# Gate and up of the first FFN by seven block products instead of eight, with weights split late

## The chip, the cores and the metric

The kernel runs on one core of a Trainium2 chip. A core has five engines that run side by side, each with an instruction queue of its own that it works off in order: TensorE (PE, matmuls), VectorE (DVE), ScalarE (ACT), GpSimd (POOL) and SyncE (SP, which issues transfers here). The metric is the device time of one execution in microseconds (us); lower is better.

## The reference

A backbone of two layers over 768 tokens (256 of context, 512 latent) with 1024 features. Layer 0 mixes the tokens by gated linear attention and differential attention side by side, layer 1 by a Mamba-2 SSD mixer on all tokens; each layer then runs a SwiGLU FFN with 2816 hidden features. Everything is fp32. The part that is changed most is the FFN of layer 0:

```python
def swiglu(h, w_in, w_out):
    gate, up = jnp.split(h @ w_in, 2, axis=-1)
    return (jax.nn.silu(gate) * up) @ w_out
...
mod_x = jax.nn.silu(c) @ mod_w[layer] + mod_b[layer]      # latent tokens
mod_c = jax.nn.silu(c_ctx) @ mod_w[layer] + mod_b[layer]  # context tokens
...
x = layer_norm(ALPHA * x + gf_x * swiglu(x * (1.0 + scf_x) + shf_x, ffn_w_in[layer], ffn_w_out[layer]),
               ln_g[layer, 1], ln_b[layer, 1])
```

The context tokens go through the same formulas with their own modulation; after layer 1 only the latent tokens are needed.

## The kernel before

**Products.** An fp32 product is three matmuls on operands that are split in a high and a low part (hi x hi, hi x lo, lo x hi; `mm3`). The activations stand split in R (768 tokens, 8 blocks of 128 features). A weight comes by a DMA of 512 KB (128x1024) into one of three buffers RAW; ScalarE copies it to the high part, and VectorE or GpSimd subtracts this from RAW to give the low part, both in RW, which has room for four weights. `issue_loads` issues the DMAs and the splits whenever `free` gives room back, and `take` hands out the next weight.

**Order.** Nothing is put in order by hand. The class `Timing` (`tm`) keeps planned times of each engine and places each instruction in them; `tm.either` puts an elementwise operation on VectorE or GpSimd, where it ends first by the plan. Side work is written as chains (Python generators, `spawn`), which `pump` lets go on between matmuls, and `need` runs a chain to its end. The program's order on each engine is the order of the planned times. All instructions are issued through one helper, so that all have line 105 in the profile; groups are told apart by their tiles.

**The FFN of layer 0** (`ffn`) has 22 hidden chunks of 128 features. `hidden(c)` computes a chunk (`gated`): gate for two groups of 384 tokens, each 8 blocks x 3 matmuls of 128x384, then up in the same way, 96 matmuls; Silu on ScalarE, the product with up on VectorE out of the PSUM tile PS, then the split of the result into the slots f. Chunks are taken in groups of three (the last of four). After a group, `out_partial` computes its part of the output product: 6 token tiles x 2 halves x 3 chunks x 3 matmuls of 128x512, 108 in all, each sum added from PS to the accumulator in HB by VectorE. The first chunk of the next group stands ahead of a group's output product.

**Beside it** run three things. The norm of the mixer's output is finished on entry (`finish`: gain and bias, 128x1024 each, for six token tiles). The modulation of layer 1 is summed (`mod_sums`: for three groups of 2048 columns, 128x1024 weights times a column of c on VectorE, once for the latent and once for the context tokens, then summed over partitions by matmuls with ONE). And late in the FFN the residual of each tile is prepared (`ln.prep`: input times ALPHA by ScalarE, gates, one 128x1024 operation), ahead of the last output product, into which the next layer's norm is woven. In layer 1's mixer the residuals are prepared in one go by the entry "p" of its order, ahead of the last quarter of the output projection.

Of the kernel before, what the change touches and what calls it, by code (L numbers as in the profile page):

```python
# [11 lines left out]
F32 = mybir.dt.float32  # L12
# [206 lines left out]
def backbone(ctx: ExitStack, tc: tile.TileContext, ins: dict, out: bass.AP):  # L219
# [20 lines left out]
    HB = pool.tile([P, NU * U], F32, name="HB")  # L240
    RAW = pool.tile([P, 3, 1024], F32, name="RAW")
    HX = pool.tile([P, 2, 1024], F32, name="HX")
# [3 lines left out]

    def unit(i, n=U):
        return HB[:, i * U:i * U + n]

# [69 lines left out]
    def pump():  # L319
        going = True  # L320
# [43 lines left out]
    plan = []  # L364
    wgate = {}
    wq = {"loaded": 0, "issued": 0, "taken": 0, "freed": 0}
    wviews = {}

    def plan_cols(key, w, c0, n=P):
        plan.append((key, [(None, w[:, c0:c0 + n].rearrange("(k p) c -> p k c", p=P))], (KD, n)))  # L370

    def plan_rows(key, w, k):
        plan.append((key, [(None, w[k * P:(k + 1) * P, :].unsqueeze(1))], (1, D)))

    def plan_halves(key, n, w, c0):
        for i in range(2):
            plan.append(((key, n, i), [(None, w[i * 512:(i + 1) * 512, c0:c0 + 256].rearrange("(k p) c -> p k c", p=P))], (4, 256)))

    def issue_loads(limit=None):
        limit = limit or len(plan)  # L380
        while wq["loaded"] < min(limit, wq["issued"] + 3):
            j = wq["loaded"]
            _, pieces, (a, b) = plan[j]
            rv = RAW[:, j % 3, 0:a * b].rearrange("p (a b) -> p a b", b=b)
            for sl, ap in pieces:
                dma(rv[:, :, sl] if sl is not None else rv, ap)
            wq["loaded"] += 1
        if wq["issued"] < min(limit, wq["freed"] + 4):
            j = wq["issued"]
            _, _, (a, b) = plan[j]  # L390
            r = RAW[:, j % 3, 0:a * b]
            i = j % 4
            hi, lo, hf = RW[:, i, 0:a * b], RW[:, 4 + i, 0:a * b], RWf[:, i, 0:a * b]
            if plan[j][0] in wgate:
                tm.either(r, r, wgate[plan[j][0]], ALU.mult)
            S.activation(hi, r, AF.Copy)
            tm.either(lo, r, hf, ALU.subtract)
            wviews[j] = hi.rearrange("p (a b) -> p a b", b=b), lo.rearrange("p (a b) -> p a b", b=b)
            wq["issued"] += 1
            issue_loads(limit)  # L400

    def take(key):
        j = wq["taken"]
        assert plan[j][0] == key, (plan[j][0], key)
        wq["taken"] += 1
        return wviews[j]

    def free(n=1):
        wq["freed"] += n
# [128 lines left out]
    def mod_sums(l, g, accs, slots, bank, tbank, pace):  # L538

        mod_bias(l, g)  # L540
        for k in range(KD):
            for hf in range(2):
                r = slots[ring("ms", len(slots))]
                c0 = g * 2048 + hf * 1024
                dma(r, mod_w[l, k * P:(k + 1) * P, c0:c0 + 1024])
                yield pace
                for m in range(2):
                    a, c = accs[2 * m + hf], CST[:, 2 * k + m:2 * k + m + 1]
                    if k == 0:
                        S.activation(a, r, AF.Copy, scale=c)  # L550
                    else:
                        V.scalar_tensor_tensor(a, r, c, a, ALU.mult, ALU.add)
        yield tuple(accs)
        o = PS[:, bank, :]
        for m in range(2):
            for j in range(4):
# [1276 lines left out]
```

## Time and profile before

| | |
|---|---|
| median of 3 runs | 2034.73 us (2030.9 to 2034.9) |
| profiled execution | 2033.6 us |
| span of its trace | 2031.7 us |
| mean granted clock of TensorE | 0.978 of full speed |
| TensorE busy | 1921.0 us |
| VectorE busy | 1352.5 us |
| ScalarE busy | 783.8 us |
| GpSimd busy | 224.5 us |

The span is the time from the first to the last instruction in the trace of one execution. A timeline row reads: start, length, engine, line, operation, tile written <- tiles read, shape, count, and in brackets the idle time before it with what ended it. A row of grouped instructions reads: group and count, then total busy time and the mean of one in ns, then the idle time before them and what ended it. RW <- RAW,RW is the low part of a weight, RW <- RAW its high part, f <- HB,f the low part of a hidden chunk, HB <- HB,CST the modulation sums, and HX <- PS,GB the modulated activations before they are split into R.

### The profile page before, as it was taken

How to read it: one execution, taken by the hardware profiler on the slowest of the kernel's cores; microseconds unless marked ns; L12 is line 12 of the kernel's file. 1: busy time of each engine (PE TensorE's matmuls, PEld its weight loads, DVE VectorE, ACT ScalarE, POOL GpSimd, SP SyncE). 2: the span in 40 equal slices, each digit the busy share in tenths (PEclk: the TensorE clock that was granted, in tenths of full speed). 3: DMA queues.
4: the chain of work that ended last, by engine and by line, in shares of the span. 5: the costliest groups of instructions: out<-in, count | busy, mean ns of one | idle time of the engine just before them, and what ended most of it. 6: DMA issues, size and time to landing. Idle time of an engine off the chain costs nothing.

```text
span 2031.7 us, 27248 instructions
## 1 busy us (share of the span) xinstructions
PE 1921.0 (95%) x10660; PEld 1650.1 (81%) x10660; DVE 1352.5 (67%) x2065; ACT 783.8 (39%) x1494; POOL 224.5 (11%) x281
## 2 busy tenths in 40 slices
PE   7999999997899999999998999999899789999997
PEld 4878787966899989899886888788788678888886
DVE  4765645588815656666478988977978884444456
ACT  3523135445423122212135465655546443222232
POOL 0100000021300000000113321401102230000010
PEclk9999999999999999999998999999999799999999
DMA  8433411122424434434323432233333325333331
GB/s 284 126 126 115 138 42 32 53 63 73 147 72 145 137 113 147 134 114 154 105 78 101 105 91 87 73 89 89 102 96 94 116 82 173 97 103 94 94 119 58
DMA packets 233071, 216.37 MB, mean 107 GB/s; under 512 B 18869, under 2 KB 202807, under 8 KB 232943
## 3 DMA queue, kind: packets, MB, share of 16 engines
q1 hardware_dynamic: 232943, 214.64, 34.4%
q8 instruction: 83, 1.36, 0.3%
q14 instruction: 45, 0.37, 0.1%
HBM read 204.94 MB, written 9.67 MB: 106 GB/s over the span
## 4 chain that ended last, share of the span: by engine, by line
PE 75%; DVE 14%; issue 3%; DMA 3%; ACT 3%; POOL 1%; SPq 0%; POOLq 0%; DVEq 0%; ACTq 0%
PE PS L105 75%; DVE HB L105 8%; DVE RW L105 2%; ACT HB L105 2%; DVE l L105 1%; DMA HB<-acs_rows 1%; DVE LNS L105 1%; ACT RW L105 1%; DMA HB<-in_x_dram 1%; DVE HX L105 1%; DVE sml L105 0%; SPq L105 0%; POOL HB L105 0%; DVE R L105 0%; POOL LNS L105 0%
## 5 line engine op out<-in xcount | busy, mean ns | idle before, releaser
L105 PE MATMUL PS<-R,RW 128*128 128x384 f32 (+3 forms) x5184 | 987.3, 349 | 19.9 <-DVE HB L105 5.8
L105 PEld LDWEIGHTS PS<-R,RW 128*128 128x128 f32 (+1 forms) x5184 | 887.3, 189 | 106.0 <-issue 20.6
L105 DVE TENSOR_TENSOR RW<-RAW,RW 128x1024 fp32r<-128x1024 f32 (+1 forms) x204 | 255.8, 1270 | 217.4 <-ACT RW L105 216.7
L105 ACT ACTIVATE RW<-RAW 128x1024 fp32r<-128x1024 f32 (+1 forms) x222 | 228.8, 1046 | 237.5 <-issue 174.5
L105 PE MATMUL PS<-RW,f 128*128 128x512 f32 x1320 | 304.7, 390 | 1.9 <-DVE RW L105 1.5
L105 ACT ACTIVATE HB<-PS 128x512 f32<-128x512 f32 (+4 forms) x247 | 129.8, 533 | 428.0 <-PE PS L105 409.7
L105 PEld LDWEIGHTS PS<-RW,f 128*128 128x128 f32 x1320 | 247.0, 188 | 55.0 <-DVE RW L105 2.1
L105 DVE TENSOR_TENSOR HB<-PS,HB 128x512 f32<-128x512 f32 (+2 forms) x276 | 160.2, 587 | 92.3 <-PE PS L105 88.7
L105 PE MATMUL PS<-RW,R 128*128 128x256 f32 (+1 forms) x1440 | 200.7, 298 | 5.4 <-DVE HB L105 4.1
L105 ACT ACTIVATE HB<-HB 128x128 f32<-128x128 f32 (+4 forms) x372 | 159.9, 488 | 102.6 <-DVE HB L105 67.5
L105 PEld LDWEIGHTS PS<-RW,R 128*128 128x128 f32 x1440 | 186.8, 196 | 14.1 <-DVE HB L105 4.9
L105 PE MATMUL PS<-RW,l 128*128 128x512 f32 x576 | 157.5, 415 | 15.5 <-DVE HX L105 6.8
L105 DVE TENSOR_TENSOR HB<-HB 128x256 f32<-128x256 f32 (+3 forms) x191 | 151.2, 802 | 21.8 <-ACT HB L105 16.3
L105 PE MATMUL PS<-HB 128*128 128x128 f32 (+6 forms) x896 | 147.2, 353 | 10.2 <-DVE HB L105 7.6
L105 PEld LDWEIGHTS PS<-RW,l 128*128 128x128 f32 x576 | 105.1, 192 | 45.5 <-DVE HX L105 8.2
L105 PEld LDWEIGHTS PS<-HB 128*128 128x128 f32 (+3 forms) x896 | 100.9, 188 | 42.5 <-DVE HB L105 12.7
L105 ACT ACTIVATE f<-HB 128x384 fp32r<-128x384 f32 (+2 forms) x68 | 37.4, 550 | 236.5 <-DVE HB L105 236.4
L105 POOL TENSOR_TENSOR HB<-HB 128x256 f32<-128x256 f32 (+1 forms) x55 | 72.8, 1334 | 504.8 <-DVE HB L105 336.1
L105 DVE TENSOR_TENSOR HB<-HB,PS 128x384 f32<-128x384 f32 (+2 forms) x68 | 39.7, 584 | 106.2 <-PE PS L105 106.2
L105 DVE SCALAR_TENSOR_TENSOR HB<-HB,CST 128x1024 f32<-128x1024 f32 x84 | 105.0, 1277 | 0.0
L105 DVE SCALAR_TENSOR_TENSOR HB<-HB,CW 128x770 f32<-128x770 f32 (+1 forms) x96 | 102.0, 1066 | 3.0
L105 PE MATMUL PS<-ident,HB 128*128 128x128 f32 x480 | 76.8, 288 | 22.5 <-DVE HX L105 11.5
(145 smaller groups left out, 1297.8 us busy)
## 6 DMA issues: line engine op xcount, KB each, us to landing
RAW<-in_ffn_w_in_dram SPq DMA_DIRECT2D x88, 512.0 KB
HB<-in_mod_w_dram SPq DMA_DIRECT2D x48, 512.0 KB
RAW<-in_ffn_w_out_dram SPq DMA_DIRECT2D x44, 512.0 KB
RAW<-in_ssd_w_in_dram SPq DMA_DIRECT2D x40, 512.0 KB
mod<-in_mod_w_dram SPq DMA_DIRECT2D x72, 256.0 KB
HB<-acs_rows SPq DMA_DIRECT2D x64, 256.0 KB
RAW<-in_ev_w_in_dram SPq DMA_DIRECT2D x20, 512.0 KB
RAW<-in_ssd_w_out_dram SPq DMA_DIRECT2D x16, 512.0 KB
```

Source lines behind the costliest of these rows:

```text
L105: f(*a, **k)
```

## The change

1. In layer 0's FFN, gate and up of the chunks 4 to 21 are computed together as a 2x2 block product: blocks of the weights are 512 input features x 128 columns of gate or up, blocks of the activations 512 features x 384 tokens. `sevenths` runs seven products of 4 blocks x 3 matmuls of 128x384 in place of eight, and combines them: three copies out of PS by ScalarE (g0, u1, g1), additions by VectorE, then Silu, product and split as before. Products 1, 5, 6, 3, 7, 2, 4 run in this order in three banks a chunk, two sets in turn.
2. Of the seven weight blocks three are blocks as loaded; four (5, 6, 3, 7) are sums or differences, built by `factor` in TW and a piece of HB. All seven are split on their own, 128x512 each. The sums of the activation blocks are built and split once (`input_sums`) into TX and a tile "sums"; the lower third of HB becomes a tile HA in the same slot, which gives place to "sums" in the FFN.
3. RW is a ring of eight single units, of which a whole weight takes two. A split that is not yet due (within two or three weights of its use) is issued only when the plan shows ScalarE and VectorE idle; `issue_loads` is asked at each `pump`.
4. The norm's finish and the input sums run as a chain (`prologue`). The residuals are prepared one by one: in layer 0 by a chain `preps`, on which the last output product waits tile by tile, in layer 1 right ahead of each tile of the last quarter of the output projection.
5. `mod_sums` takes weights of 128x512 and sums the context tokens' row in the first group only, which holds the shift and scale ahead of layer 1's mixer; the context rows of the other two groups enter nothing.

```diff
+    FACTORS = "1563724"
...
+    def plan_pair(key, w, c0, c1):
+        for c in (c0, c1):
+            j = load(w[:, c:c + P].rearrange("(k p) c -> p k c", p=P), (KD, P))
+        for f in FACTORS:
+            items.append(((key, f), 1, j, f))
+    def factor(f, j):
+        w = [[RAW[:, (j - 1 + i) % 3, k * 512:(k + 1) * 512] for k in range(2)] for i in range(2)]
+        if f in "124":
+            return {"1": w[0][0], "2": w[0][1], "4": w[1][1]}[f]
+        r = TW[f in "67"]
+        a, b, op = {"5": (w[1][0], w[1][1], ALU.add), "6": (TW[0], w[0][0], ALU.subtract),
+                    "3": (w[0][1], TW[1], ALU.subtract), "7": (w[0][0], w[1][0], ALU.subtract)}[f]
+        tm.either(r, a, b, op)
+        return r
...
-        if wq["issued"] < min(limit, wq["freed"] + 4):
...
+            late = n >= max(upto, wq["taken"] + (2 if f is None else 3))
...
+                if late and not idle(r, *v):
+                    return
...
-        for k in range(KD):
-            for hf in range(2):
-                r = slots[ring("ms", len(slots))]
-                c0 = g * 2048 + hf * 1024
-                dma(r, mod_w[l, k * P:(k + 1) * P, c0:c0 + 1024])
+        for js, ms in ((((0, 1), (0, 1)), ((2, 3), (0, 1))) if g == 0 else (((0, 1, 2, 3), (0,)),)):
+            for k in range(KD):
+                for i, j in enumerate(js):
+                    r = slots[ring("ms", len(slots))]
+                    c0 = g * 2048 + j * 512
+                    dma(r, mod_w[l, k * P:(k + 1) * P, c0:c0 + 512])
...
+        def sevenths(c):
+            n = ring("sets", 2)
+            o1, o2, o3 = (PS[:, 3 * n + i, 0:N2] for i in range(3))
...
+            prod("1", o1, True)
+            S.activation(g0, o1, AF.Copy)
+            prod("5", o3, True)
+            S.activation(u1, o3, AF.Copy)
+            prod("6", o1)
+            S.activation(g1, o1, AF.Copy)
+            prod("3", o3)
+            V.tensor_tensor(g1, o3, g1, ALU.add)
+            S.activation(g1, g1, AF.Silu)
+            prod("7", o1)
+            V.tensor_tensor(u1, o1, u1, ALU.add)
+            tm.either(u1, u1, g1, ALU.mult)
+            store(u1, slice(N2, 2 * N2))
+            prod("2", o2, True)
+            V.tensor_tensor(g0, o2, g0, ALU.add)
+            S.activation(g0, g0, AF.Silu)
+            need(*sums)
+            prod("4", o1)
+            V.tensor_tensor(g0, o1, g0, ALU.mult)
+            store(g0, slice(0, N2))
...
-        for t in tiles:
-            lnin.finish(t)
+        def prologue():
+            for t in tiles:
+                lnin.finish(t, l == 0)
+                if l == 0:
+                    yield 2.4
+            if l == 0:
+                yield from input_sums(True)
...
-                        for t in tiles:
-                            ln.prep(t)
+                        def preps():
+                            for t in tiles:
+                                ln.prep(t)
+                                prepped.add(t)
+                                yield 4.0
...
-                for t in range(2, NT):
-                    ln.prep(t)
...
+                    if i == 3:
+                        ln.prep(t)
```

A product "6", "3" or "7" goes into a bank without clearing it (`start` false), so it adds to what the product before left there.

What stands in the engines' queues at the places that the prediction speaks of follows; the numbers behind tile names are buffer numbers. TensorE, around a chunk of layer 0's FFN, before (f are the hidden chunks in an output product, R_69 the split activations):

```order
L105 MATMUL PS<-RW,f_4_3787 128x512 x3
L105 MATMUL PS<-RW,f_0_3783 128x512 x3
L105 MATMUL PS<-R_69,RW 128x384 x249
L105 MATMUL PS<-HB,ONE 32x512 x8
L105 MATMUL PS<-R_69,RW 128x384 x9
```

And after, from the end of an output product on:

```order
L105 MATMUL PS<-RW,f_0_3780 128x512 x3
L105 MATMUL PS<-R_69,RW 128x384 x12
L105 MATMUL PS<-TX,RW 128x384 x12
L105 MATMUL PS<-sums_4057,RW 128x384 x12
L105 MATMUL PS<-R_69,RW 128x384 x12
L105 MATMUL PS<-sums_4057,RW 128x384 x12
L105 MATMUL PS<-R_69,RW 128x384 x36
L105 MATMUL PS<-TX,RW 128x384 x12
```

One long run over several chunks has become products of 12: 1, 5, 6, 3, 7, then 2, 4 and the next chunk's 1 as one row of 36.

VectorE in the same chunks, before:

```order
L105 TENSOR_TENSOR HB<-HB,PS 128x384
L105 TENSOR_TENSOR f_0_3783<-HB,f_0_3783 128x384
L105 SCALAR_TENSOR_TENSOR HB<-HB,CST 128x1024
L105 TENSOR_TENSOR HB<-HB,PS 128x384
L105 TENSOR_TENSOR f_0_3783<-HB,f_0_3783 128x384
L105 TENSOR_TENSOR RW<-RAW,RW 128x1024
```

And after (HB<-RAW, TW<-HB,RAW and HB<-RAW,TW are block sums of weights):

```order
L105 TENSOR_TENSOR HB<-RAW 128x512
L105 TENSOR_TENSOR TW<-HB,RAW 128x512
L105 TENSOR_TENSOR RW<-HB,RW 128x512
L105 TENSOR_TENSOR RW<-TW,RW 128x512
L105 TENSOR_TENSOR HB<-RAW,TW 128x512
L105 TENSOR_TENSOR HB<-PS,HB 128x384
L105 TENSOR_TENSOR RW<-HB,RW 128x512
L105 SCALAR_TENSOR_TENSOR HB<-HB,CST 128x512
L105 TENSOR_TENSOR HB<-PS,HB 128x384
L105 TENSOR_TENSOR HB<-HB 128x384
L105 SCALAR_TENSOR_TENSOR HB<-HB,CST 128x512
L105 TENSOR_TENSOR f_1_3781<-HB,f_1_3781 128x384
```

More and smaller operations stand between those that read PS.

VectorE at the entry of layer 0's FFN, where HX <- PS,GB is awaited by TensorE, before:

```order
L105 BN_STATS LNS<-HB 128x6
L105 TENSOR_TENSOR RW<-RAW,RW 128x1024 x2
L105 TENSOR_SCALAR HX<-PS,GB 128x128
```

And after:

```order
L105 BN_STATS LNS<-HB 128x6
L105 TENSOR_TENSOR RW<-RAW,RW 128x1024
L105 TENSOR_SCALAR HX<-PS,GB 128x128
```

One low part of a weight has left its place.

VectorE in layer 1, ahead of its last output projection, before (HB<-HB 128x1024 are the residuals; l is a part of the SSD's output that TensorE waits for):

```order
L105 TENSOR_TENSOR HB<-HB 128x1024
L105 TENSOR_TENSOR HB<-PS,HB 128x512
L105 TENSOR_TENSOR HB<-HB 128x256 x2
L105 TENSOR_TENSOR HB<-PS,HB 128x256
L105 TENSOR_TENSOR HB<-PS,HB 128x512
L105 TENSOR_TENSOR HB<-HB 128x256 x2
L105 TENSOR_TENSOR HB<-PS,HB 128x256
L105 SCALAR_TENSOR_TENSOR DS<-HB,CBD 128x4
L105 TENSOR_TENSOR HB<-HB 128x1024
L105 SCALAR_TENSOR_TENSOR l_4_7581<-l_4_7581,PS 128x512
```

And after:

```order
L105 TENSOR_TENSOR GB<-GB,MODS 128x8
L105 TENSOR_TENSOR RW<-RAW,RW 128x1024
L105 TENSOR_TENSOR HA_7515<-PS,HB 128x512
L105 TENSOR_TENSOR HA_7515<-HA_7515 128x256 x2
L105 TENSOR_TENSOR HA_7515<-PS,HA_7515 128x256
L105 SCALAR_TENSOR_TENSOR l_4_7810<-l_4_7810,PS 128x512
```

The residuals no longer stand ahead of l <- l,PS; a weight's low part does.

More of the change, by code (lines that the diff above doesn't have):

```diff
@@ L360, in mm3, with load, plan_load @@
         mm(o, ll, rh, False, stop)
-    plan = []
+    loads, items = [], []
     wgate = {}
-    wq = {"loaded": 0, "issued": 0, "taken": 0, "freed": 0}
+    wq = {"loaded": 0, "used": 0, "issued": 0, "units": 0, "taken": 0, "freed": 0, "room": 8, "limit": 0}
     wviews = {}
+    FACTORS = "1563724"
+    def load(ap, shape):
+        loads.append((ap if isinstance(ap, list) else [(None, ap)], shape))
+        return len(loads) - 1
+    def plan_load(key, ap, shape):
+        items.append((key, 2, load(ap, shape), None))
@@ L379, in issue_loads @@
[L379 to L387, printed above, removed]
-        if wq["issued"] < min(limit, wq["freed"] + 4):
[L389 to L398, printed above, removed]
+            plan_load((key, n, i), w[i * 512:(i + 1) * 512, c0:c0 + 256].rearrange("(k p) c -> p k c", p=P), (4, 256))
@@ new lines, in idle, with issue_loads @@
+    def idle(r, hi, lo):
+        n = math.prod(r.shape[1:])
+        c = [tm.COST[e][0] + tm.COST[e][1] * n for e in "SV"]
+        t = tm.room("S", max(tm.ready(r, 1), tm.free(hi, 1), tm.clock - 10.0), c[0]) + c[0]
+        t = max(t, tm.free(lo, 1))
+        return tm.room("V", t, c[1], True) <= max(t, tm.clock) + 0.1
+    def issue_loads(upto=0):
+        limit = wq["limit"]
+        while True:
+            while wq["loaded"] < min(limit, wq["used"] + 3, len(loads)):
+                j = wq["loaded"]
+                pieces, (a, b) = loads[j]
+                rv = RAW[:, j % 3, 0:a * b].rearrange("p (a b) -> p a b", b=b)
+                for sl, ap in pieces:
+                    dma(rv[:, :, sl] if sl is not None else rv, ap)
+                wq["loaded"] += 1
+            n = wq["issued"]
+            if n >= min(limit, len(items)) or wq["units"] + items[n][1] > wq["room"] or items[n][2] >= wq["loaded"]:
+                return
+            key, units, j, f = items[n]
+            u = wq["units"] % 8
+            late = n >= max(upto, wq["taken"] + (2 if f is None else 3))
+            if f is None:
+                a, b = loads[j][1]
+                r = RAW[:, j % 3, 0:a * b]
+                v, vf = ([x[:, i, 0:a * b] for i in (u, (u + 1) % 8)] for x in (RW, RWf))
+                if late and not idle(r, *v):
+                    return
+                if key in wgate:
+                    tm.either(r, r, wgate[key], ALU.mult)
+                split(v[0], v[1], r, vf[0])
+                wq["used"] += 1
+            else:
+                b = P
+                v, vf = ([x[:, u, i * 512:(i + 1) * 512] for i in range(2)] for x in (RW, RWf))
+                if late and not idle(RAW[:, (j - 1) % 3, 0:512] if f in "12" else RAW[:, j % 3, 0:512], *v):
+                    return
+                split(v[0], v[1], factor(f, j), vf[0])
+                wq["used"] += 2 * (f == FACTORS[-1])
+            wviews[n] = tuple(x.rearrange("p (a b) -> p a b", b=b) for x in v)
@@ L399, in issue_loads @@
             wq["issued"] += 1
-            issue_loads(limit)
+            wq["units"] += units
     def take(key):
-        j = wq["taken"]
-        assert plan[j][0] == key, (plan[j][0], key)
+        n = wq["taken"]
+        assert items[n][0] == key, (items[n][0], key)
+        issue_loads(n + 1)
         wq["taken"] += 1
-        return wviews[j]
+        return wviews[n]
     def free(n=1):
-        wq["freed"] += n
+        for _ in range(n):
+            wq["room"] += items[wq["freed"]][1]
+            wq["freed"] += 1
@@ L702, in out_partial @@
                 if ln is not None:
+                    while ln.prepped is not None and t not in ln.prepped:
+                        need_one()
                     ln.last(t, hf, o)
@@ L1225, in hid @@
         def hid(c):
+            if l == 0 and c >= 4:
+                plan_pair(("fs", l, c), w_in, c * P, HID + c * P)
+                return
             plan_cols(("fg", l, c), w_in, c * P)
```

211 lines of the change are left out of this document (158 added, 53 removed).

## The prediction

> **What bounds the kernel now.** I read the page's engine lines first, then the chain of work that ended last, then TensorE's timeline in layer 0's FFN, and then the other engines' load there.
>
> ```profile
> span 2031.7 us, 27248 instructions
> ...
> PE 1921.0 (95%) x10660; PEld 1650.1 (81%) x10660; DVE 1352.5 (67%) x2065; ACT 783.8 (39%) x1494; POOL 224.5 (11%) x281
> ...
> PE 75%; DVE 14%; issue 3%; DMA 3%; ACT 3%; POOL 1%; SPq 0%; POOLq 0%; DVEq 0%; ACTq 0%
> ```
>
> TensorE is busy for 95% of the span and makes up 75% of the chain. In the chain by time, one piece covers the changed stage:
>
> ```profile
> 527.18 513.74 PE PS L105 x2780
> 1041.96 1.05 ACT RW L105
> 1043.03 1.24 DVE RW L105
> ```
>
> From 527 to 1041 us nothing but TensorE is on the chain, 2780 matmuls in a row. So each matmul left out there shortens the kernel by its own length, as long as the other engines keep up with the shorter stream. The timeline gives the lengths:
>
> ```profile
> 610.88 50.11 PE L105 MATMUL PS<-R,RW 128*128 128x384 f32 x288
> 660.82 24.68 PE L105 MATMUL PS<-RW,f 128*128 128x512 f32 x108
> ...
> 728.62 1.92 PE L105 MATMUL PS<-HB,ONE 128*32 128x512 f32 x16
> ...
> 1044.31 6.00 PE L105 MATMUL PS<-RW,f 128*128 128x512 f32 x25 [0.76 <-DVE RW L105]
> ```
>
> 288 matmuls of gate and up take 50.11 us, 0.174 us each (three hidden chunks of 96); a block product of 12 will take 2.09 us. The output product's matmul takes 24.68/108 = 0.2285 us.
>
> Next, how much room the engines around TensorE have, in that stage and in a busier one (layer 1's mixer). The columns are window, length, then busy time of PE, PEld, DVE, ACT and POOL, the granted clock, DMA share and GB/s:
>
> ```profile
> 528.00:1040.00 512.00, 512.00 (x2771) 481.21 (x2770) 294.42 (x327) 131.96 (x186) 17.96 (x10) 1.00 0.40 127
> 1110.00:1400.00 290.00, 276.91 (x1664) 241.47 (x1663) 251.47 (x393) 167.62 (x356) 60.57 (x99) 0.98 0.34 96
> ```
>
> In the FFN VectorE is busy for 294.4 of 512 us (57%) and TensorE never idles. In the mixer VectorE is busy for 251.5 of 290 us (87%), and TensorE idles for 13.1 us, 4.5%. The second row is my measure of what a full VectorE costs.
>
> **The change, part by part.** The sum is made against the profiled execution, 2033.6 us; the median of the runs, 2034.73, is 1.1 us above it.
>
> *Fewer products.* Chunks 4 to 21 are 18 chunks. Each has 7 block products of 12 matmuls, 84, where there were 96. 18 x 12 = 216 matmuls go, at 0.174 us: **-37.6 us**. They are of the same shape as those that stay, so no end of this term is open.
>
> *Fewer sums of the modulation.* For two of three groups only the latent row is summed, and 8 of 24 fp32 matmuls go, which the profile counts as 16 passes: **-1.9 us** by the 728.62 row. Their weights come in twice as many DMAs of half the size. The stage's DMA share is 0.40 and nothing there waits for a transfer, so the 48 more DMA issues on SP cost nothing; if that cover went, what would be late is the sums, due only at the FFN's end.
>
> *More work on VectorE, GpSimd and ScalarE in the FFN.* These are the prices:
>
> ```profile
> L105 DVE TENSOR_TENSOR RW<-RAW,RW 128x1024 fp32r<-128x1024 f32 x203 | 255.4, 1274 | 211.6 <-ACT RW L105 210.9
> ...
> L105 DVE TENSOR_TENSOR HB<-PS,HB 128x512 f32<-128x512 f32 x164 | 112.3, 687 | 80.4 <-PE PS L105 80.2
> L105 DVE SCALAR_TENSOR_TENSOR HB<-HB,CST 128x1024 f32<-128x1024 f32 x84 | 105.0, 1277 | 0.0
> ...
> L105 DVE TENSOR_TENSOR HB<-HB 128x512 f32<-128x512 f32 x40 | 29.2, 735 | 1.8 <-ACT HB L105 0.7
> ...
> L105 DVE TENSOR_TENSOR HB<-HB,PS 128x384 f32<-128x384 f32 x44 | 24.3, 553 | 54.2 <-PE PS L105 54.2
> ...
> L105 ACT ACTIVATE HB<-PS 128x384 f32<-128x384 f32 x69 | 33.8, 491 | 169.4 <-PE PS L105 157.3 <-DVE HB L105 12.0
> ...
> L105 ACT ACTIVATE R<-HX 128x512 fp32r<-128x512 f32 x32 | 19.8, 628 | 26.7 <-DVE HX L105 26.2
> ...
> L105 DVE SCALAR_TENSOR_TENSOR HB<-PS,RS,HB 128x512 f32<-128x512 f32 x24 | 17.8, 742 | 1.8 <-POOL RS L105 1.6
> ...
> L105 POOL TENSOR_TENSOR RW<-RAW,RW 128x512 fp32r<-128x512 f32 x1 | 1.5, 1482 | 0.5 <-ACT RW L105 0.5
> ```
>
> A chunk before had two low parts of weights (1.274 each) and four elementwise operations of 384 columns (0.553). Now it has 7 low parts and 4 block sums of 128x512 (0.735) and 7 elementwise operations. Over 18 chunks: 198 operations of 0.735 us, of which the order puts 45 on GpSimd, leaves 153, 112.5 us; the elementwise ones are 126 x 0.553 = 70 us; out go 36 x 1.274 = 45.9 and 72 x 0.553 = 40 us. The modulation sums go from 105.0 us to 112 of half width, about 83 (at 0.742, as other operations of this kind and width take). The sums of the input blocks, prologue and later, are 26 operations of 768 columns, 1.10 us each by the 0.735 row, 4 on GpSimd: 24 us. VectorE then has 294 + 112.5 + 70 - 45.9 - 40 - 22 + 24 = 393 us of work in some 473 us, 83%. GpSimd gets 45 x 1.482 = 66.7 us where it had 18. ScalarE gets per chunk seven copies at 0.63 (the 628 ns row, of the same width) for two at 1.05, and three copies of 0.491 out of PSUM: 69 us more on 132, 42%, no bound.
>
> So no engine is full on average, and what is left is waits. Before, a product's operands were ready long before it. Now, by the order, about five products of a chunk start when only one product, 2.09 us, stands between them and the one whose bank must be read out first (0.491 on ScalarE, 0.553 on VectorE). Alone that fits; behind a split and a block sum on an in-order VectorE (0.735 + 0.735 + 0.553 = 2.02) it just fits. The bounds are 0 and 4.5% of 473 us, 21 us, the mixer's rate. The mixer's waits are chains over several engines, these are one operation with a cover, so I take a third: **+7 us**.
>
> *Bank at a group's edge.* In three places (chunks 7, 13 and 19) the chunk's first product goes into the bank that the output product's last sum still has to be read from (0.687, and two handovers). Before, six banks rotated. About 1 us each, **+3 us** (0 to 6).
>
> *Splits late.* A low part is now made two or three items before its use, and at the last output product two of them have only 7 and 10 matmuls (1.6 and 2.3 us) to cover 1.05 + 1.24 us. The 1044.31 row shows that the same place waited 0.76 already. **+1 us** (0 to 3). At the entry of the FFN one split fewer stands ahead of what TensorE waits for:
>
> ```profile
> 519.10 0.66 PE L105 MATMUL PS<-ident,HB 128*128 128x128 f32 x4 [1.62 <-DVE HX L105]
> ...
> 516.38 2.35 DVE L105 TENSOR_TENSOR RW<-RAW,RW 128x1024 fp32r<-128x1024 f32 x2
> 518.64 0.41 DVE L105 TENSOR_SCALAR HX<-PS,GB 128x128 f32<-128x128 f32 x1
> ...
> 520.96 1.22 DVE L105 TENSOR_TENSOR RW<-RAW,RW 128x1024 fp32r<-128x1024 f32 x1
> ```
>
> The x2 becomes one, 1.2 us earlier here, and the next split at 520.96 also moves back: **-2 us** (-3 to 0). Elsewhere in the mixers splits move both ways. At the entry of layer 1 both splits still stand ahead of the awaited operations, so I take 0 for the rest. A split costs 1.27 us where it is ahead of an awaited operation and 2.3 us (1.05 + 1.24) where it comes too late; with eight such places in one direction that is -10 to +18 us at the very ends.
>
> *Residuals one by one.* In layer 0 three of them (128x1024, 1.23 us) now run inside the last output product, where VectorE is nearly full: **+3 us** (0 to 4). In layer 1 they leave the queue ahead of an awaited operation:
>
> ```profile
> 1614.13 0.69 PE L105 MATMUL PS<-ident,l 128*128 128x128 f32 x2 [10.88 <-DVE l L105]
> ...
> 1593.58 4.82 DVE L105 TENSOR_TENSOR HB<-HB 128x1024 f32<-128x1024 f32 x4
> ...
> 1602.20 2.49 DVE L105 TENSOR_TENSOR HB<-HB 128x1024 f32<-128x1024 f32 x1 [1.63 <-ACT HB L105]
> ...
> 1611.32 1.23 DVE L105 TENSOR_TENSOR HB<-HB 128x1024 f32<-128x1024 f32 x1 [0.48 <-ACT HB L105]
> 1612.46 0.68 DVE L105 SCALAR_TENSOR_TENSOR l<-l,PS 128x512 f32<-128x512 f32 x1
> ```
>
> TensorE waits 10.88 us for the last row, behind six residuals, 8.54 us, which no longer stand there; one more split (1.24) does. They come back among the last output projection, where five are on GpSimd. I take **-5 us**, about half of the wait, since the operations behind the residuals wait for other engines too (-10.9 to +3).
>
> *Norm pass and input sums.* They run beside 336 matmuls of chunks 0 to 3 at the start, where VectorE is half idle: 0; without that cover 24 us.
>
> Sum: -37.6 - 1.9 + 7 + 3 + 1 - 2 + 3 - 5 = -32.5. 2033.6 - 32.5 = **2001 us**.
>
> **The rivals.** *A. More comes back in the mixers.* The 10.88 us wait goes whole (-5.9 more) and the splits give their 10 us: 1985 us. For it: the pieces of the chain that are VectorE's splits. Against it: only one of the places that I compared in the order loses one.
>
> *B. VectorE at the mixer's rate of waits.* 21 us for 7: 2015 us. For it: 83% against 87%. Against it: the short chains.
>
> *C. GpSimd stops VectorE (the other side).* One operation on VectorE, beside a GpSimd split and alone:
>
> ```profile
> 504.55 0.81 DVE L105 TENSOR_SCALAR HB<-HB,LNS 128x1024 f32<-128x1024 f32 x1 [0.47 <-POOL LNS L105]
> ...
> 510.85 2.96 DVE L105 TENSOR_SCALAR HB<-HB,LNS 128x1024 f32<-128x1024 f32 x1 [0.62 <-POOL LNS L105]
> ...
> 510.88 2.38 POOL L105 TENSOR_TENSOR RW<-RAW,RW 128x1024 fp32r<-128x1024 f32 x1
> ```
>
> It takes 2.96 us, not 0.81, and ends after GpSimd's. If each of the 45 new GpSimd operations holds VectorE so, VectorE has 393 + 67 = 460 of 473 us, and its queue passes every delay on to the next product. The sum without waits in the FFN is 1994; so the change is slower once 40 of the 66.7 us reach TensorE, 0.31 us for each of 126 products. With two thirds of them it is 1994 + 44 = 2038, with all 2061. Against it: a delay of 1.48 us is inside the 2.09 us of one product, and the mixer has 60.6 us of GpSimd in 290 and idles for 4.5%. The Trainium skill states this as a rule ("SBUF — State Buffer", section "SBUF: two separate sides"): VectorE and GpSimd share a pair of ports under an exclusive lock, held for the whole instruction, and a VectorE operation in a 2-port mode takes it, and one with two SBUF inputs too against a GpSimd operation that reads SBUF. By that rule all 153 splits and block sums are open to it, and case C's 2038 would be the time; the 510.85 row agrees with the blocking, and the mixer's row says that not much of it reaches TensorE.
>
> That the products do not get fewer is excluded: the order shows 7 runs of 12 in each changed chunk.
>
> **How the numbers follow.** Forecast as summed (1992 to 2010): 0.58. A (1982 to 1992): 0.18. B (2010 to 2029): 0.17. C: 0.07, of which 0.02 ends within 0.2% of before. 0.2%, 4 us, is about what a measurement of this kernel can tell from no change. Faster by more: 0.58 + 0.18 + 0.16 = 0.92; within: 0.03; slower: 0.05. The range of 8 in 10 cuts off the lower part of A and the upper part of B with C: 1985 to 2018 us.
>
> **What would show it.** TensorE's matmuls of 128x384 fall by 216; the stage that takes 513.7 us now takes 474 to 495; VectorE is at 80 to 86% in it and GpSimd at 15 to 20%. Waits of TensorE for VectorE's HB and RW and ScalarE's HB appear there, under 0.5 us each and some 7 us in all. In layer 1 the 10.88 us wait is 4 to 8. Wrong would be: waits in the FFN above 20 us (B or C, told apart by stretched VectorE operations beside GpSimd's), waits for late splits in the mixers, or a stage in which gate and up still run without a gap while the time goes elsewhere.

## The result: slower by 0.8%, where 1.6% faster was forecast

| | before | changed |
|---|---|---|
| median of 4 runs | 2033.23 us | 2047.98 us (2046.62 to 2051.79) |
| ratio | | 1.0076 (95%: 1.0058 to 1.0095) |
| profiled execution | 2033.6 us | 2048.03 us |

The page of the changed kernel, the lines that answer to those of before:

```profile
span 2046.0 us, 27426 instructions
...
PE 1898.2 (93%) x10428; PEld 1619.9 (79%) x10428; DVE 1481.4 (72%) x2263; ACT 852.3 (42%) x1650; POOL 358.8 (18%) x353
...
PE 62%; DVE 25%; ACT 4%; issue 4%; DMA 3%; POOL 1%; SPq 1%; POOLq 0%; DVEq 0%; ACTq 0%
```

TensorE is busy for 22.8 us less, but the span is 14.3 us longer: VectorE's share of the chain went from 14% to 25%. Two windows of the changed kernel, the FFN from its first full products to its last chunk and a stretch of layer 1, and the stretch of layer 1 before (busy time of PE, PEld, DVE, ACT, POOL, then the granted clock):

```profile
531.00:1026.00 495.00, 483.64 (x2553) 447.47 (x2551) 394.09 (x540) 192.41 (x334) 88.42 (x56) 1.00 0.41 126
1150.00:1250.00 100.00, 86.70 (x498) 73.89 (x497) 90.49 (x133) 56.32 (x134) 40.63 (x45) 0.95 0.25 72
```

```profile
1150.00:1250.00 100.00, 94.39 (x591) 82.39 (x589) 88.01 (x147) 59.05 (x143) 23.70 (x40) 1.00 0.31 88
```

In the FFN VectorE has the 394 us of work that were forecast, and the stage is 18 us shorter. In layer 1, whose products the change leaves as they were, GpSimd is busy for 40.6 us in place of 23.7, and TensorE for 7.7 us less. TensorE's granted clock is 0.95 there, for 1.00 before. Over the thousand matmuls from the 4400th to the 3400th from the end, a stretch that holds this window, TensorE idles for 23.2 us in place of 9.8 and is busy for 170.2 in place of 167.7: most of the loss is waiting, and some 2.5 us are the same matmuls at a mean granted clock of 0.956 for 0.971.

To see where the time went I compare the two timelines of TensorE at places where the same number of matmuls has been done from the start, or is still to come (all matmuls of layer 1 and the second FFN are the same in both, though their order moves a little). "n to come" is counted to the end. The places at 4500 and 2400 to come lie in long runs of the same matmuls, where no kernel waits. A value is good to some 4 us: two of the kernels below run the same instructions up to there, and stood 4.4 us apart after 3250 matmuls.

| stretch | forecast | changed minus before | low parts on VectorE minus before | splits early minus before |
|---|---|---|---|---|
| start to the FFN's first chunks (3250 done) | -2 | +7.0 | -4.0 | -0.3 |
| FFN's groups, to 5000 to come | -29.5 | -23.2 | -23.4 | -15.9 |
| last output product, entry of layer 1, to 4500 to come | +4 | +15.1 | +12.8 | +16.9 |
| layer 1 to ahead of its tail, 2400 to come | 0 | +12.8 | +13.1 | +3.1 |
| tail of layer 1, 1500 to come | -5 | +2.4 | -1.4 | +0.9 |
| rest | 0 | +0.3 | +0.4 | +0.3 |
| sum | -32.5 | +14.4 | -2.5 | +5.0 |

(The last two columns are experiments below, in one profiled execution each; that of the first was 3.5 us above its median. Their expectations quote a stretch that ends at 4700 to come, as 60.6 us before and 82.3. Counted matmul by matmul it is 58.8 and 72.0, and 70.6 in the changed kernel; that end lies among waits which stand in another order in each kernel, so I go by 4500, where the stretch is 106.9 us before, 122.0 changed, and 119.8 with low parts on VectorE.)

### The profile page after: what moved, and what is told of

The parts are those of the page before. It is cut to its first block, busy times and chain, and to the rows that moved or that the text cites. A ratio compares the mean times of both kernels' runs of the same rounds, so it can differ in the third digit from the quotient of the medians.

```text
span 2046.0 us, 27426 instructions
## 1 busy us (share of the span) xinstructions
PE 1898.2 (93%) x10428; PEld 1619.9 (79%) x10428; DVE 1481.4 (72%) x2263; ACT 852.3 (42%) x1650; POOL 358.8 (18%) x353
## 4 chain that ended last, share of the span: by engine, by line
PE 62%; DVE 25%; ACT 4%; issue 4%; DMA 3%; POOL 1%; SPq 1%; POOLq 0%; DVEq 0%; ACTq 0%
PE PS L105 62%; DVE HB L105 12%; DVE HA L105 4%; DVE RW L105 3%; ACT HB L105 2%; DVE l L105 2%; DVE LNS L105 1%; DVE sml L105 1%; ACT RW L105 1%; DMA HA<-acs_rows 1%; DVE HX L105 1%; ACT HA L105 1%; DMA HB<-in_mod_w_dram 1%; SPq L105 1%; DMA mod<-in_mod_w_dram 0%
## 5 line engine op out<-in xcount | busy, mean ns | idle before, releaser
L105 PE MATMUL PS<-R,RW 128*128 128x384 f32 (+3 forms) x4320 | 850.7, 353 | 30.8 <-DVE HB L105 10.1
L105 PEld LDWEIGHTS PS<-R,RW 128*128 128x128 f32 (+1 forms) x4320 | 741.7, 190 | 119.2 <-issue 20.1
L105 DVE TENSOR_TENSOR RW<-RAW,RW 128x1024 fp32r<-128x1024 f32 (+2 forms) x189 | 218.1, 1166 | 129.6 <-ACT RW L105 127.9
L105 ACT ACTIVATE RW<-RAW 128x1024 fp32r<-128x1024 f32 (+2 forms) x240 | 225.0, 951 | 135.8 <-issue 69.5
L105 ACT ACTIVATE HB<-PS 128x384 f32<-128x384 f32 (+5 forms) x196 | 109.2, 560 | 244.3 <-PE PS L105 240.3
L105 DVE TENSOR_TENSOR HB<-PS,HB 128x512 f32<-128x512 f32 (+1 forms) x204 | 129.3, 639 | 81.1 <-PE PS L105 80.4
L105 POOL TENSOR_TENSOR RW<-RAW,RW 128x1024 fp32r<-128x1024 f32 (+1 forms) x51 | 114.0, 2239 | 202.8 <-ACT RW L105 194.8
L105 DVE SCALAR_TENSOR_TENSOR HB<-HB,CST 128x512 f32<-128x512 f32 x112 | 94.8, 862 | 7.6 <-DMA HB<-in_mod_w_dram 7.6
L105 ACT ACTIVATE HA<-HA,HB 128x128 f32<-128x128 f32 x256 | 80.0, 392 | 28.6 <-DMA HA<-acs_rows 28.4
L105 PE MATMUL PS<-sums,RW 128*128 128x384 f32 x432 | 81.3, 335 | 2.1 <-ACT HB L105 2.1
```

Of the source, the lines that this page charges most:

```text
L105: f(*a, **k)
```

## The experiments

Each differs from the changed kernel unless it says otherwise. Theory P: low parts of weights that the planner now gives to GpSimd hold VectorE, and with it TensorE. Rivals: the lateness of the splits itself (L), the block products' load in the FFN (B), the FFN's residuals (R). The kernel before ran anew beside each group of experiments, at medians of 2033.2 to 2035.8 us; so a difference between experiments of two groups is good to 2 or 3 us, and where the ratios to before give another one, it stands beside.

**Whole weights' low parts on VectorE.**

```diff
-                split(v[0], v[1], r, vf[0])
+                S.activation(v[0], r, AF.Copy)
+                V.tensor_tensor(v[1], r, vf[0], ALU.subtract)
```

> The changed kernel, with splits as late as there, but the low parts of whole weights (128x1024) always on VectorE: 184 there and none on GpSimd. Theory P: VectorE gets 34 x 1.27 = 43 us more work, but its operations in layer 1 are no longer stretched; layer 1 gets 10 to 14 of its lost 16 us back: 2034 to 2038 us. Theory L: the splits are as late as before and VectorE is fuller: 2048 or more. Rival B: 2048.

Measured: 2027.38 us, ratio to before 0.9972 (0.9963 to 0.9981). That one subtraction's engine turns the change from a loss into a gain: 20.6 us, the most of any single edit that leaves the work complete. The rule for when a split is due is the same and VectorE is given more to do, so lateness and load by themselves do not make these 20 us. The edit also moves what the planner places after it, and the table shows where it helps: 11 us at the FFN's entry and 4 in layer 1's tail. In layer 1 ahead of that the sum does not change, +13.1 us for +12.8: from 4400 to 3400 to come 10.4 us are gained (193.4 to 183.0), and 10.3 are lost just ahead of it.

The mechanism in layer 1, from 4400 to 3400 to come, on VectorE, GpSimd and TensorE of the changed kernel:

```profile
1175.31 6.54 DVE L105 SCALAR_TENSOR_TENSOR HB<-HB,CW 128x770 f32<-128x770 f32 x4 [0.73 <-ACT HB L105]
...
1195.40 2.91 DVE L105 TENSOR_TENSOR HA<-HA 128x256 f32<-128x256 f32 x2
...
1176.31 2.38 POOL L105 TENSOR_TENSOR RW<-RAW,RW 128x1024 fp32r<-128x1024 f32 x1 [4.95 <-ACT RW L105]
...
1195.42 2.62 POOL L105 TENSOR_TENSOR RW<-RAW,RW 128x1024 fp32r<-128x1024 f32 x1
...
1184.29 0.88 PE L105 MATMUL PS<-ident,HB 128*128 128x128 f32 x6 [1.79 <-DVE HB L105]
...
1199.88 2.29 PE L105 MATMUL PS<-R,RW 128*128 128x256 f32 x9 [4.10 <-DVE l L105]
```

The same operations before:

```profile
1171.72 4.18 DVE L105 SCALAR_TENSOR_TENSOR HB<-HB,CW 128x770 f32<-128x770 f32 x4
...
1191.42 0.89 DVE L105 TENSOR_TENSOR HB<-HB 128x256 f32<-128x256 f32 x2
```

Four convolution steps take 6.54 us in place of 4.18, with a low part on GpSimd inside them; two operations of 256 columns take 2.91 for 0.89, beginning 0.02 us ahead of one. TensorE waits behind both. Counted in the timelines, 23 of layer 1's low parts are on GpSimd now and 9 were before.

What is lost ahead of it are waits for VectorE, one of them for a low part (TensorE, then VectorE, of the kernel with low parts on VectorE):

```profile
1130.03 5.96 PE L105 MATMUL PS<-RW,R 128*128 128x256 f32 x35 [3.23 <-DVE RW L105]
...
1123.76 4.13 DVE L105 SCALAR_TENSOR_TENSOR HB<-HB,CW 128x770 f32<-128x770 f32 x4
...
1128.75 1.22 DVE L105 TENSOR_TENSOR RW<-RAW,RW 128x1024 fp32r<-128x1024 f32 x1
```

The low part comes behind four convolution steps; just before, TensorE waits 3.5 us for l. From 4500 to 4400 to come, where neither the kernel before nor the changed one waits, TensorE idles for 6.8 us in this kernel, and its 100 matmuls are busy for 18.2 us at a granted clock of 0.86, where they take 14.6 us at 1.00 in the other two.

It also undoes the loss at the FFN's entry. The changed kernel (TensorE, VectorE, GpSimd):

```profile
529.85 1.97 PE L105 MATMUL PS<-ident,HB 128*128 128x128 f32 x8 [7.76 <-DVE HX L105]
...
522.83 6.63 DVE L105 TENSOR_TENSOR RW<-RAW,RW 128x1024 fp32r<-128x1024 f32 x2
529.39 0.72 DVE L105 TENSOR_SCALAR HX<-PS,GB 128x128 f32<-128x128 f32 x2
...
519.97 8.43 POOL L105 TENSOR_TENSOR HB<-HB,HA 128x1024 f32<-128x1024 f32 x3
```

And with the low parts on VectorE:

```profile
522.11 1.09 PE L105 MATMUL PS<-ident,HB 128*128 128x128 f32 x8 [1.55 <-DVE HX L105]
...
519.38 2.35 DVE L105 TENSOR_TENSOR RW<-RAW,RW 128x1024 fp32r<-128x1024 f32 x2
...
516.52 2.39 POOL L105 TENSOR_TENSOR HB<-HB,HA 128x1024 f32<-128x1024 f32 x1
```

The two splits stand ahead of the awaited HX <- PS,GB in both. They take 6.63 us beside a train of three norm operations on GpSimd, and 2.35 us where the order leaves only one there, ahead of them. So what blocks here is no low part on GpSimd; it is low parts on VectorE that are blocked. The Trainium skill's page "SBUF — State Buffer" (section "SBUF: two separate sides") has the rule for it, an exclusive lock for the whole instruction between the two engines; these rows agree. The kernel before had the same train, beside other operations; so had the next kernel, whose splits are early again:

```profile
523.60 7.97 POOL L105 TENSOR_TENSOR HB<-HB,HA 128x1024 f32<-128x1024 f32 x3
...
526.91 1.09 PE L105 MATMUL PS<-ident,HB 128*128 128x128 f32 x8 [1.17 <-DVE HX L105]
```

There TensorE waits 1.17 us at the same place for 7.76. At the entry it is thus the splits' later place, inside the train, that cost the time; taking them out or moving the train both repair it.

**Splits issued early.**

```diff
-            late = n >= max(upto, wq["taken"] + (2 if f is None else 3))
+            late = False
```

> The changed kernel, but a weight's split is issued as soon as there is room for it, due or not. By the order GpSimd then makes 17 low parts of whole weights, as before the change, where the changed kernel gives it 34. Theory P (a low part on GpSimd takes 2.6 us and holds VectorE's operations beside it; it is the engine that matters, not the lateness): layer 1 between its 4400th and 3400th matmul from the end, which lost 16 us, gets most of it back; about 2034 us. Theory L (the lateness itself, splits that arrive after they are wanted): the same 2034, and the two are told apart by the next kernel. Rival B (the block products, through the load on VectorE and GpSimd in the FFN, are the whole loss): no gain, 2048.

Measured: 2037.82 us, 1.0026 (1.0014 to 1.0038). Ten of the 20 us come back, with 17 low parts on GpSimd instead of 34. From 4400 to 3400 to come it takes 180.4 us, where before took 177.5, the changed kernel 193.4, and late splits with none on GpSimd 183.0: two different ways to take them off GpSimd both repair this stretch. Early splits do not have the waits ahead of it either, so of layer 1's 12.8 us 3.1 are left here. This edit changes the lateness and the engine together, and the two are not parted by it. What early splits lose is in the FFN, 16 us gained there in place of 23.

**The cause by itself, in the kernel before.** One kernel with all low parts on VectorE, one with 23 of layer 1's on GpSimd and the rest on VectorE:

```diff
-            tm.either(lo, r, hf, ALU.subtract)
+            V.tensor_tensor(lo, r, hf, ALU.subtract)
```

```diff
-            tm.either(lo, r, hf, ALU.subtract)
+            l1 = plan[j][0][0] in ("cv", "z", "sw")
+            (G if l1 and j % 5 in (0, 2) else V).tensor_tensor(lo, r, hf, ALU.subtract)
```

> The kernel before, with all low parts of weights on VectorE, of which GpSimd had 17 there. If a low part on GpSimd costs as much there as in the changed kernel (some 20 us for 34): 2023 to 2028 us. If it is the changed order that makes it costly: 2031 to 2036 us.

> The kernel before with 23 low parts of layer 1's whole weights on GpSimd, as many as the changed kernel has there, and all others on VectorE; nothing else is changed. Its counterpart with none on GpSimd took 2037.9 us and 174.7 us from the 4400th to the 3400th matmul from the end, with operations of 770 columns on VectorE at 1.05 us. Theory P (a low part on GpSimd holds VectorE): these operations go to 1.25 us or more, the stretch to 185 to 195 us, the time to 2048 to 2060 us. Rival (the changed kernel's order of layer 1 is slow for another reason): within 4 us of 2038, the stretch under 180 us.

Measured: 2037.92 us, 1.0016 (1.0005 to 1.0027), and 2053.39 us, 1.0080 (1.0065 to 1.0095). Against each other 15.5 us for 23 low parts (13.0 by the ratios), 0.6 to 0.7 us each; the changed kernel's 20.6 us for 34 are 0.61 each. The time is as Theory P forecast; its other two signs missed. The stretch from 4400 to 3400 to come takes 178.5 us against 175.3, where 185 to 195 were expected and the rival had under 180, and the convolution steps do not reach 1.25 us. The loss is later in layer 1: the two kernels' timelines lie 3.6 us apart at 3100 to come and 11.8 at 2300. Seventeen on GpSimd by the planner's choice cost the kernel before nothing (with none it is a little slower, which neither range of that expectation held); whether it is their number or their place that costs in the other two, the runs do not part.

What the 23 do to VectorE shows when its other operations in layer 1 (4700 to 1500 to come) are compared group by group, the same operation, tiles and shape in both: they take 29.5 us longer than with none on GpSimd, 1.3 us for each low part moved, while GpSimd's own other work there is no longer (105 us for 110). A low part that takes 1.27 us on VectorE thus costs VectorE as much when GpSimd does it. In the changed kernel it is 47.9 us for the 24 of that stretch, where GpSimd's other work also grew by 14 us, and in the kernel before 16.6 us for its 10, which do not reach the time there. The convolution steps' rows, in the groups kept apart by shape, of before:

```profile
L105 DVE SCALAR_TENSOR_TENSOR HB<-HB,CW 128x770 f32<-128x770 f32 x80 | 90.3, 1129 | 2.6
```

of the changed kernel:

```profile
L105 DVE SCALAR_TENSOR_TENSOR HB<-HB,CW 128x770 f32<-128x770 f32 x80 | 102.7, 1284 | 5.1 <-ACT HB L105 2.3
...
L105 POOL TENSOR_TENSOR RW<-RAW,RW 128x1024 fp32r<-128x1024 f32 x34 | 89.1, 2622 | 155.6 <-ACT RW L105 147.5 <-ACT ea L105 6.6 <-PE PS L105 1.3
```

of the changed kernel with low parts on VectorE:

```profile
L105 DVE SCALAR_TENSOR_TENSOR HB<-HB,CW 128x770 f32<-128x770 f32 x80 | 84.5, 1058 | 6.9 <-ACT HB L105 4.3
```

and of the kernel before with 23 on GpSimd:

```profile
L105 DVE SCALAR_TENSOR_TENSOR HB<-HB,CW 128x770 f32<-128x770 f32 x80 | 90.8, 1137 | 6.5 <-ACT HB L105 3.8
```

The same 80 operations mean 1058 ns with none of layer 1's low parts on GpSimd, 1129 with 9, 1284 with 23; the forced 23 (1137) hardly slowed these and met others, such as the 20 steps HB <- HB of the same width, which mean 1233 ns for 1061 with none. So the price falls on whatever runs beside.

**No block products.**

```diff
-            if l == 0 and c >= 4:
+            if l == 0 and c >= 99:
```

(in both places; the input sums are left out.)

> The changed kernel without the block products: chunks 4 to 21 are computed by eight products of whole weights as before, and the input sums are left out; late splits, norm pass, residuals one by one and the smaller modulation sums stay. If the block products themselves gain (my reading of the trace: 22 us over their six groups) and the loss is elsewhere: 2048 + 22 = 2070 us, less what they cost at the FFN's ends (up to 10), so 2060 to 2070. Rival B (the block products are the whole loss): 2031 to 2035.

Measured: 2063.03 us, 1.0148 (1.0128 to 1.0169). The block products gain 15 us net of what they cost at the FFN's ends; rival B falls. The last output product and the entry of layer 1, from 5000 to 4500 to come, take 110.5 us here, 106.9 before and 122.0 in the changed kernel: that loss needs the block products beside the residuals. Layer 1 up to 2400 to come loses 19.8 us here without any block product, with 30 low parts on GpSimd in all: that loss does not need them.

**Block work on VectorE** (with low parts on VectorE; the block sums and their low parts too).

```diff
-        tm.either(r, a, b, op)
-        return r
+        V.tensor_tensor(r, a, b, op)
+        return r
```

> As the kernel with whole low parts on VectorE (2027.4 us), and the block sums of weights and their low parts (128x512), 43 of which it has on GpSimd, are all on VectorE too. In the FFN's six groups of block products that kernel is 14 us above the sum of its products. If GpSimd's lock makes these waits: half comes back, 2018 to 2022 us. If VectorE's load makes them (it gets 43 x 0.7 = 30 us fuller, 90% of the stage): 2030 to 2040 us.

Measured: 2043.72 us, 1.0044 (1.0029 to 1.0059), 16 us worse (14.6 by the ratios). In the FFN GpSimd's help is worth more than its blocking costs, but not by much: the FFN's groups take 3.7 us more. The worst new wait stands at their end:

```profile
1007.06 6.15 PE L105 MATMUL PS<-R,RW 128*128 128x384 f32 x24 [7.43 <-DVE HB L105]
```

Most of the loss is not there: of the 10 us between the two profiled executions 6.7 are in layer 1, whose order the planner places after the FFN's. Why they are lost is open.

**The FFN's residuals.** In one go:

```diff
-                                yield 4.0
...
-                        spawn(preps(), 3.0)
+                        preps()
```

> The changed kernel, but the FFN's residuals are prepared in one go at the place where their chain starts, with the one buffer that the change leaves them. Theory R1 (one by one they come into the last output product and hold ScalarE's splits there; 13 us were lost from that product to the entry of layer 1): 5 to 8 us come back, 2040 to 2043 us. Theory R2 (it is the single buffer, each load waiting for the tile before): 2047 to 2050 us.

Measured: 2056.69 us, 1.0118 (1.0102 to 1.0135), worse than either theory had it, but it shows how the loads hold TensorE at its plainest (TensorE, then ScalarE):

```profile
1047.48 0.80 PE L105 MATMUL PS<-RW,f 128*128 128x512 f32 x1 [19.37 <-ACT RW L105]
...
1034.14 1.06 ACT L105 ACTIVATE HB<-HB 128x1024 f32<-128x1024 f32 x1 [4.64 <-DMA HB<-xres]
1039.67 1.06 ACT L105 ACTIVATE HB<-HB 128x1024 f32<-128x1024 f32 x1 [4.48 <-DMA HB<-xres]
1045.43 1.06 ACT L105 ACTIVATE HB<-HB 128x1024 f32<-128x1024 f32 x1 [4.70 <-DMA HB<-xres]
1046.39 1.99 ACT L105 ACTIVATE RW<-RAW 128x1024 fp32r<-128x1024 f32 x2
```

The change left the residuals one buffer where there were two (its LN takes b[0:1] for LNB[0:2]). A load now waits for the tile before it; ScalarE stands for four of the six loads here, 14.3 us in all, and the two splits that TensorE needs stand behind. In the changed kernel it stands for three, 10.9 us, and before the change 0.43 us for one. One by one, as changed, the same row is shorter:

```profile
1033.89 0.59 PE L105 MATMUL PS<-RW,f 128*128 128x512 f32 x1 [4.96 <-ACT RW L105]
...
1031.84 1.06 ACT L105 ACTIVATE HB<-HB 128x1024 f32<-128x1024 f32 x1 [2.38 <-DMA HB<-xres]
1032.80 1.99 ACT L105 ACTIVATE RW<-RAW 128x1024 fp32r<-128x1024 f32 x2
```

Ahead of it stand three gate products on VectorE beside three on GpSimd:

```profile
1013.84 5.77 DVE L105 TENSOR_TENSOR HB<-HB 128x1024 f32<-128x1024 f32 x3
...
1015.19 10.01 POOL L105 TENSOR_TENSOR HB<-HB 128x1024 f32<-128x1024 f32 x3 [9.84 <-DMA HB<-gates]
```

Four more kernels, all on top of the one with low parts on VectorE, took this apart. A chunk earlier, with denser modulation sums (`c == c0 + n + 1`, pace 3.0 for 3.4):

> As the kernel with whole low parts on VectorE (2027.4 us), and the FFN's residuals start one chunk earlier (after chunk 19, not 20), with the modulation sums paced a little faster so that they end before. From the 5000th to the 4700th matmul from the end that kernel took 82.3 us, the kernel before 60.6. Theory R3 (the residuals have one block chunk of 14.6 us, in which VectorE already has 12 us of work, and so push ScalarE's splits and the chunk's own operations behind them): 10 to 15 us come back, 2012 to 2018 us. Rival R2 (the single buffer, each load behind the last): 2025 to 2028.

Measured: 2059.14 us, 1.0117 (1.0096 to 1.0139). Both theories missed: against the kernel that it was made from, the FFN's groups take 15.5 us more, most of it before a second residual is even loaded, beside the denser sums, and the wait for ScalarE's splits stays (5.71 us). The edit changed two things, so it says nothing about the residuals' place. In halves of 512 columns, two to the buffer:

> As the kernel with whole low parts on VectorE (2027.4 us); the FFN's residuals of layer 0 are loaded, scaled and added in halves of 512 columns, so that the one buffer works as two half ones and a load need not wait for the whole tile before. Theory R2 (the single buffer: ScalarE stands for the residual's load, 14.1 us in four waits, ahead of the two splits that TensorE then waits 5.2 us for): the 5.2 us wait goes to under 2, 4 to 8 us come back, 2019 to 2023 us. Rival R3 (VectorE has too much to do beside chunk 21): 2026 to 2031 us.

Measured: 2036.7 us, 1.0015 (1.0001 to 1.0029). The wait went from 5.18 to 2.50 us, but the stretch from 5000 to 4500 to come stays (118.7 us for 119.8), since others grew, and the time is longer, by 9 us. It decides nothing. Off ScalarE:

```diff
-            S.activation(xr, xr, AF.Copy, scale=ALPHA)
...
-            tm.either(y, y, xr, ALU.add)
+            V.scalar_tensor_tensor(y, xr, ALPHA, y, ALU.mult, ALU.add)
```

> As the kernel with whole low parts on VectorE (2027.4 us); the FFN's residuals of layer 0 are scaled and added in one operation of VectorE, so that ScalarE does not wait for their loads ahead of the splits. If that queue order on ScalarE makes the 5.2 us wait: it goes, 2020 to 2024 us. If the loads are what is late, VectorE now stands for them ahead of its own work: 2027 to 2035 us.

Measured: 2025.1 us, 0.9948 (0.9930 to 0.9967), the fastest version that computes everything; the stretch takes 114.4 us for 119.8, though layer 1 took more again in the profiled execution. Of 5.18 us for ScalarE's splits 1.60 are left, and VectorE is late next:

```profile
1019.76 0.50 PE L105 MATMUL PS<-RW,f 128*128 128x512 f32 x1 [1.60 <-ACT RW L105]
1023.48 13.03 PE L105 MATMUL PS<-RW,f 128*128 128x512 f32 x47 [3.21 <-DVE RW L105]
...
1071.61 3.46 PE L105 MATMUL PS<-R,RW 128*64 128x384 f32 x10 [6.20 <-DVE RW L105]
```

With that, and layer 1's first four low parts given to either engine again:

> As the kernel with the residual off ScalarE (2025.1 us), and the low parts of layer 1's first four weights are given again to the engine that ends first by the plan, since GpSimd is free there and VectorE is behind the norm: TensorE waited there 6.2 us for a low part on VectorE. If that engine is the cause: the wait falls to 1 to 3 us, and 3 to 5 us come back, 2020 to 2023 us. If VectorE's norm operations are what TensorE waits for next: 2024 to 2027 us.

Measured: 2028.06 us, 0.9973 (0.9963 to 0.9984): no gain over the last, 3 us slower (5 by the ratios). The 6.20 us wait is gone, and others stand in its place:

```profile
1061.35 0.39 PE L105 MATMUL PS<-R,RW 128*64 128x384 f32 x1 [2.46 <-ACT R L105]
1063.43 0.90 PE L105 MATMUL PS<-R,RW 128*64 128x384 f32 x2 [1.69 <-DVE R L105]
1077.67 0.66 PE L105 MATMUL PS<-ident,HB 128*128 128x128 f32 x4 [3.52 <-DVE HX L105]
```

And with the residuals left out:

> As the kernel with whole low parts on VectorE (2027.4 us), with the residuals of layer 0's FFN left out (no load, scaling, gate product or addition; the output is another one). From the 5000th to the 4700th matmul from the end it took 82.3 us for 60.6 before the change. If the residuals beside chunk 21 make this loss: 62 to 70 us there, and 2008 to 2016 us in all. If it is the entry of layer 1 (low parts behind the norm): over 76 us, and 2022 us or more.

Measured: 2016.9 us, 0.9930 (0.9909 to 0.9950). The stretch from 5000 to 4500 to come takes 105.8 us, 106.9 before the change and 119.8 with the residuals: the whole loss there, 13 us, goes with them. The time is 10.5 us shorter than with them, a little above the range that gave them the loss. One wait stands at the entry of layer 1 even so, but the stretch as a whole is no slower than before, which waits in other places there (TensorE idles for 10.0 us before, 10.8 here):

```profile
1058.07 3.46 PE L105 MATMUL PS<-R,RW 128*64 128x384 f32 x10 [6.29 <-DVE RW L105]
```

**Layer 1's residuals in one go** (again by the entry p; with low parts on VectorE).

```diff
+                for t in range(2, NT):
+                    ln.prep(t)
...
-                    if i == 3:
-                        ln.prep(t)
```

> As the kernel with whole low parts on VectorE (2027.4 us), but layer 1's residuals are prepared in one go by the entry p, as before the change. My prediction gave their move 5 us: 2030 to 2034 us. Rival (another wait takes the place of the 10.88 us one, as the changed kernel's trace has it: the stretch from the 2000th to the 1700th matmul from the end took 71.3 us for 74.9): 2027 to 2031 us.

Measured: 2032.82 us, 0.9988 (0.9976 to 0.9999): 5.4 us slower than its base (3.3 by the ratios).

## Why the prediction was wrong

*Fewer products and sums.* Right: the FFN's stage of 513 us is 495, and the kernel without block products is slower. The forecast for the FFN's groups, -29.5 us with their waits, was 6 us too good; their waits, as the time between two matmuls' starts beyond the usual, are some 15 us in place of 10. VectorE's 393 us and GpSimd's 15 to 20% were met (394 us; 88.4 of 495 us, 18%). The waits were forecast as many, under 0.5 us each; TensorE's rows name few and longer ones, 11 us in 11 waits:

```profile
PE PS L105 <- DVE HB L105: 8.9, 9, 2.2
PE PS L105 <- ACT HB L105: 2.1, 2, 1.4
```

*Splits late, the part "I take 0 for the rest".* This step failed, by 13 us in layer 1. I looked whether splits still stand ahead of awaited operations in VectorE's queue, and not at which engine the moved ones land on. The order showed it: GpSimd's list has 34 low parts of whole weights for 17. What the runs showed in place of 0 are two costs: a low part on GpSimd holds VectorE (10 us from 4400 to 3400 to come), and VectorE, where it has them all and late, holds TensorE itself (10 us just ahead of that, in part for a low part). Undoing the lateness, and with it the moves to GpSimd, leaves 3.1 of the 13 us; undoing the engine alone leaves all of them, in another place.

*Splits late, -2 at the FFN's entry.* Failed by 9 us. One split did leave its place, and the two behind it fell beside GpSimd's norm operations, a train that was there before. With the low parts on VectorE the stretch is at -4.0, with early splits at -0.3.

*Rival C, GpSimd stops VectorE, chance 0.07.* The mechanism was right, and the sign with it. Its place was wrong: I priced it only for the 45 new block operations in the FFN, where taking GpSimd away made things worse, and argued from a mixer that was measured with 9 low parts on GpSimd that it would not matter much. That the measured time lies near its 2038 us is luck: the delay came from other operations, in other stages.

*Residuals one by one, +3, and the last product's splits, +1.* Failed by 11 us (+15.1 for +4), the second largest miss, and the residuals are the whole of it: without them the stretch is no longer than before. I costed instructions, not the buffer: the diff cuts the residuals' buffers from two to one, and ScalarE stands 10.9 us for their loads at the head of its queue. I also took chunk 21 as cover that it no longer is, 14.6 us long with 12 us of VectorE's work of its own. How much is the buffer's and how much the gate products' beside that chunk is not shown: no kernel with two buffers was run, and taking the wait off ScalarE brought 5 us of the 13.

*Layer 1's residuals, -5.* Right in size: undoing it costs 3 to 5 us. But the tail came out at +2.4 us, and at -1.4 with low parts on VectorE. In the changed kernel the gain is hidden, as the 10.88 us wait gave way to three:

```profile
1567.34 9.28 PE L105 MATMUL PS<-RW,l 128*128 128x512 f32 x27 [4.44 <-DVE l L105]
...
1620.66 0.44 PE L105 MATMUL PS<-ident,l 128*128 128x128 f32 x2 [3.66 <-DVE l L105]
...
1633.78 1.10 PE L105 MATMUL PS<-l,HA 128*128 128x64 f32 x8 [3.21 <-DVE HA L105]
```

Open stays how the 15 us of waits in the FFN's groups divide between VectorE's load and the blocking by GpSimd, how much of layer 1's 13 us is lateness by itself, and what the planner's new order, which moves with every edit, adds to each difference.

## What to carry to other kernels

Where a planner chooses between two engines that block each other, count which engine each moved operation lands on, everywhere in the program and not only where the change is: here one subtraction's engine was worth 20.6 us, more than the 15 us that the block products brought. Then look where an edit's gain falls: this one's 20 us came at the entry and the tail, and hid a new loss of 10 us in the middle. Read a diff's buffer counts like its instructions; a ring cut from two to one can put a load's wait at the head of an in-order queue. Compare two timelines at places where no kernel waits, or a wait that has only moved looks like a loss. A stage that covered side work before must be measured again after it has been made shorter and fuller.

## What was not expected of the hardware

A low part of a weight on GpSimd, 2.5 us of an idle engine's time, cost the whole kernel 0.6 to 0.7 us (20.6 us for 34, 13 to 15.5 us for 23), and VectorE itself 1.3 us of longer operations (29.5 us for 23), where doing it itself takes 1.27. And the blocking goes both ways: three gate products on GpSimd take 10.01 us beside three on VectorE that take 5.77, where one takes 2.52 on GpSimd in the mean before, and 1.23 alone on VectorE.
